# Attention over 32 sequences of different length on one core: hardware loops synchronised by counting registers in place of loop stages with semaphore resets, and one output store per sequence

## The chip, the cores and the metric

The kernel runs on one core of a Trainium2 chip. The metric is the device time of one execution in microseconds (us). Before the change the median of three runs is 631.83 us (626.99 to 632.2 us). One execution was profiled; it took 629.71 us, and the profile's span, from its first to its last instruction, is 627.9 us.

Engines are named as the profile names them: PE is the matrix engine and PEld its weight loads, DVE the vector engine, ACT the scalar engine, POOL the GpSimd engine, SP the engine whose queue here issues all DMA transfers. A name with a q behind it (PEq, SPq) is that engine's sequencer, the part that reads instructions, computes registers and waits on semaphores.

## The reference

```python
batch, max_seq, n_heads, head_dim = (32, 512, 8, 64)
lengths = np.random.randint(64, max_seq, size=batch)
x: [32, 512, 512] float32      w_qkv: [512, 1536] float32

output = np.zeros_like(x)
for b in range(batch):
    seq_len = lengths[b]
    x_b = x[b, :seq_len].copy()
    qkv = np.matmul(x_b, w_qkv)
    q, k, v = np.split(qkv, 3, axis=-1)        # then 8 heads of 64
    ...
    scores = scale * np.matmul(q, k.transpose(0, 2, 1))
    attn = np.exp(scores - scores_max)
    attn = attn / (np.sum(attn, axis=-1, keepdims=True) + 1e-08)
    output[b, :seq_len] = np.matmul(attn, v)   # heads side by side again
```

Every sequence is projected to q, k and v, attended within its own length, and written; rows behind its length are zero in the output.

## The kernel before, in words

**Order of the sequences.** The 32 sequences are ranked on the chip by length, longest first (L59 to L100). A place in that ranking is called a position. A position needs n tiles of 128 rows, n from 4 down to 1. The kernel counts on the chip how many pairs of positions need more than 3, 2 and 1 tiles (`pair_i`, L103 to L112), and it has one hardware loop for each n (L362 and L363), whose first and last pair are read from those counts. With the lengths of this case the loops run 2 iterations at n = 4, 6 at n = 3, 6 at n = 2 and 2 at n = 1, each of them two positions.

**One iteration.** For j = 0 and 1 an iteration merges two lists of steps (L366 to L369): the attention of position 2p+j, and the QKV projection of the position after it, whose x was loaded earlier. The buffers for x, x in 16 bits, its transpose, q, k, v, the output tile and the mask are doubled and alternate with j.

- Projection: POOL casts the n tiles of x to 16 bits (`prep`, L196 to L200), and SP then loads the x of a later position into the freed buffer (L178). PE transposes (L205), ACT copies the transpose out of PSUM (L208), PE multiplies by the weights (L213 for q and k, L230 for v), DVE copies q (L225), k (L221) and v (L237) out of PSUM.
- Attention: DVE copies the position's mask (L262). For each pair of heads and each key tile PE computes scores (L275) and ACT takes their exponentials (L282). For each head PE multiplies by v, which carries a column of ones for the sum (L294), and DVE takes the reciprocal, multiplies it by the row mask and scales the result into the output tile `out_nat` (L302, L303, L306).
- Store (L313 to L317): SP stores the n computed tiles, and for n < 4 stores the remaining 4 - n tiles of the position from a constant tile `zeros`, cleared once by POOL (L155, L156). In the built program the second of these transfers waits until the first has landed. An iteration's last instructions on SP are these two transfers of its position j = 1.

**The loops.** `iteration_sync="staggered"` (L363) cuts a loop body into four stages. Each stage has its own semaphores, which are set back for the next iteration, so that every wait of the body is against a constant. An engine, SP with the transfers of that stage among them, reports that it has left a stage; an engine may enter a stage only when all have left the stage two before it. Between two loops all engines meet at a barrier twice: once when the loop is left, and, after each engine has loaded the next bounds into registers, once before the next is entered.

Of the kernel before, what the change touches and what calls it, by code (L numbers as in the profile page):

```python
# [9 lines left out]
FP32 = mybir.dt.float32  # L10
# [3 lines left out]
ALU = mybir.AluOpType  # L14
AX = mybir.AxisListType

P = 128
# [6 lines left out]
def kernel(  # L24
# [8 lines left out]
    nc = tc.nc  # L33
    B, MAXS, D = x.shape
    NT = MAXS // P
# [5 lines left out]
    const = ctx.enter_context(tc.tile_pool(name="const", bufs=1))  # L41
# [8 lines left out]
    for c in range(NC):  # L50
# [23 lines left out]
        out=cmp,  # L74
        in0=key.unsqueeze(1).broadcast_to([P, B, B]),
        in1=key.unsqueeze(2).broadcast_to([P, B, B]),
        op=ALU.is_gt,
# [5 lines left out]
        out=hit,  # L83
        in0=rank.unsqueeze(1).broadcast_to([P, B, B]),
        in1=idx_f.unsqueeze(2).broadcast_to([P, B, B]),
        op=ALU.is_equal,
    )
    nc.vector.tensor_tensor(
        out=cmp, in0=hit, in1=idx_f.unsqueeze(1).broadcast_to([P, B, B]), op=ALU.mult
# [7 lines left out]
        out=hit, in0=hit, in1=len_f.unsqueeze(1).broadcast_to([P, B, B]), op=ALU.mult  # L97
# [8 lines left out]
    for t in range(1, NT):  # L106
        nc.vector.tensor_scalar(
            out=more[:, t - 1, :], in0=first, scalar1=float(t * P), scalar2=None, op0=ALU.is_gt
# [13 lines left out]
        out=masks[:, 0:B, 1, :],  # L122
        in0=iota_f.unsqueeze(1).broadcast_to([P, B, NT]),
        in1=slen.unsqueeze(2).broadcast_to([P, B, NT]),
        op=ALU.is_lt,
    )
    nc.vector.tensor_scalar(
        out=masks[:, 0:B, 0, :],
        in0=masks[:, 0:B, 1, :],
# [6 lines left out]
    def ring(n, shape, dtype, name, fill=None, pool=const):  # L136
        got = []
        for k in range(n):
            t = pool.tile(shape, dtype, name=f"{name}{k}")
            if fill is not None:  # L140
                nc.gpsimd.memset(t, fill)
            got.append(t)
        return got
# [4 lines left out]
    x_bufs = ring(2, [P, NT, D], FP32, "x_nat")  # L148
    x16_bufs = ring(2, [P, NT, D], F16, "x16")
    xT_bufs = ring(2, [P, NC, MAXS], F16, "xT")  # L150
    o_bufs = ring(2, [P, NT, D], FP32, "out_nat")
    m_bufs = ring(2, [P, 2, NT], FP32, "mask")
    e_bufs = ring(4, [P, 2, NT, MAXS], F16, "et")
    rcp_bufs = ring(4, [P, NT], FP32, "rcp")
    zeros = const.tile([P, NT - 1, D], FP32)  # L155
    nc.gpsimd.memset(zeros, 0.0)  # L156

    g_bufs = ring(2, [P, MAXS], FP32, "g", pool=ps)
    s_bufs = ring(2, [P, 2, MAXS], FP32, "psc", pool=ps)
# [4 lines left out]
    ov = out.rearrange("b (t p) d -> b p t d", p=P)  # L164
# [25 lines left out]
    def qkv_steps(b, n, at):  # L190

        steps = []
        N = n * P
        x16, xT, kT = x16_bufs[b % 2], xT_bufs[b % 2], k_bufs[b % 2]

        def prep():  # L196
            for t in range(n):
                nc.gpsimd.tensor_copy(out=x16[:, t, :], in_=x_bufs[b % 2][:, t, :])  # L198
            if at is not None:
                dma_x(b % 2, at, n)  # L200

        def trans(c):
            pxt = nxt("g", gx_bufs)
            for t in range(n):
                nc.tensor.transpose(  # L205
                    pxt[:, t * P : (t + 1) * P], x16[:, t, c * P : (c + 1) * P], ident_f16
                )
            nc.scalar.copy(out=xT[:, c, 0:N], in_=pxt[:, 0:N])  # L208

        def qk(m):  # L210
            pq = nxt("g", g_bufs)
            for c in range(NC):
                nc.tensor.matmul(  # L213
                    pq[:, 0:N],
                    w_r[:, c, m * P : (m + 1) * P],
                    xT[:, c, 0:N],
                    start=(c == 0),
                    stop=(c == NC - 1),
                )
            if m >= NC:  # L220
                nc.vector.tensor_copy(out=kT[:, m - NC, 0:N], in_=pq[:, 0:N])  # L221
            else:
                for par in range(2):
                    r = slice(HD * par, HD * (par + 1))
                    nc.vector.tensor_copy(out=q_bufs[b % 2][r, m, par, 0:N], in_=pq[r, 0:N])  # L225

        def val(t):
            pv = nxt("g", g_bufs)
            for c in range(NC):
                nc.tensor.matmul(  # L230
                    pv,
                    xT[:, c, t * P : (t + 1) * P],
                    w_r[:, c, 2 * D : 3 * D],
                    start=(c == 0),
                    stop=(c == NC - 1),
                )
            nc.vector.tensor_copy(  # L237
                out=v_bufs[b % 2][:, t, :, 0:HD], in_=pv.rearrange("p (h d) -> p h d", d=HD)
            )

        steps.append(prep)
        for c in range(NC):
            steps.append(lambda c=c: trans(c))
        for m in (0, 4, 1, 5, 2, 6, 3, 7):
            steps.append(lambda m=m: qk(m))
        for t in range(n):
            steps.append(lambda t=t: val(t))
        return steps

    def attn_steps(b, n, at, pos):  # L250

        N = n * P
        kT = k_bufs[b % 2]
        qz = q_bufs[b % 2]
        v_aug = v_bufs[b % 2]
        o_t = o_bufs[b % 2]
        mask = m_bufs[b % 2]
        etp = [None] * (NH // 2)
        steps = []

        def masking():
            nc.vector.tensor_scalar(  # L262
                out=mask,
                in0=masks[:, bass.ds(pos, 1), :, :].rearrange("p o m t -> p (o m) t"),
                scalar1=0.0,
                scalar2=None,
                op0=ALU.add,
            )

        def scores(i, kt):  # L270
            if kt == 0:
                etp[i] = nxt("e", e_bufs)
            psc = nxt("s", s_bufs)
            for par in range(2):
                nc.tensor.matmul(  # L275
                    psc[:, par, 0:N],
                    kT[:, i, kt * P : (kt + 1) * P],
                    qz[:, i, par, 0:N],
                    start=True,
                    stop=True,  # L280
                )
            nc.scalar.activation(  # L282
                out=etp[i][:, :, kt, 0:N],
                in_=psc[:, :, 0:N],
                func=AF.Exp,
                scale=scale,
                bias=mask[:, 0, kt : kt + 1],
            )

        def av(h):  # L290
            pav = nxt("o", pav_bufs)
            for qt in range(n):
                for kt in range(n):
                    nc.tensor.matmul(  # L294
                        pav[:, qt, :],
                        etp[h // 2][:, h % 2, kt, qt * P : (qt + 1) * P],
                        v_aug[:, kt, h, :],
                        start=(kt == 0),
                        stop=(kt == n - 1),
                    )  # L300
            rcp = nxt("r", rcp_bufs)
            nc.vector.reciprocal(out=rcp[:, 0:n], in_=pav[:, 0:n, HD])  # L302
            nc.vector.tensor_tensor(  # L303
                out=rcp[:, 0:n], in0=rcp[:, 0:n], in1=mask[:, 1, 0:n], op=ALU.mult
            )
            nc.vector.tensor_tensor(  # L306
                out=o_t[:, 0:n, h * HD : (h + 1) * HD],
                in0=pav[:, 0:n, 0:HD],
                in1=rcp[:, 0:n].unsqueeze(2).broadcast_to([P, n, HD]),
                op=ALU.mult,  # L310
            )

        def store():  # L313
            to = ov[bass.ds(at, 1), :, :, :].rearrange("o p t d -> (o p) t d")
            nc.sync.dma_start(out=to[:, 0:n, :], in_=o_t[:, 0:n, :])
            if n < NT:
                nc.sync.dma_start(out=to[:, n:NT, :], in_=zeros[:, 0 : NT - n, :])  # L317

        steps.append(masking)
        for i in range(NH // 2):  # L320
            if i > 0:
                got = [lambda kt=kt, i=i: scores(i, kt) for kt in range(n)]
                ave = [lambda h=h: av(h) for h in (2 * i - 2, 2 * i - 1)]
                steps += merge(got, ave)
            else:
                steps += [lambda kt=kt: scores(0, kt) for kt in range(n)]
        steps.append(lambda: av(6))
        steps.append(lambda: av(7))
        steps.append(store)
        return steps  # L330

# [12 lines left out]
    firsts = [0]  # L344
# [15 lines left out]
        step()  # L360

    for k, n in enumerate(range(NT, 0, -1)):  # L362
        with tc.For_i(firsts[k], firsts[k + 1], iteration_sync="staggered") as p:  # L363
            pos = p * 2
            for j in range(2):
                proj = qkv_steps(1 - j, n, batch_at(pos + (3 + j)))  # L366
                att = attn_steps(j, n, batch_at(pos + j), pos + j)
                for step in merge(att, proj):
                    step()  # L369
# [35 lines left out]
```

## Time and profile before

| | |
|---|---|
| median of three runs | 631.83 us (626.99 to 632.2) |
| profiled execution, and its span | 629.71 us, 627.9 us |
| PE busy | 474.2 us, 76% of the span, 4160 matmuls |
| PE weight loads busy | 291.6 us, 46%, 4160 |
| DVE busy | 403.0 us, 64%, 1301 instructions |
| ACT busy | 312.7 us, 50%, 457 |
| POOL busy | 60.9 us, 10%, 99 |
| HBM read and written | 27.30 MB and 33.55 MB, 97 GB/s over the span |
| mean granted PE clock | 0.910 of full speed |

Busy time is an average over a prologue, four loops of different shape and the turns between them. To see what a stage is limited by, the same counts are read for one iteration at a time (a table by stretches of time), and the turns between iterations are read in the timeline, instruction by instruction. The "idle before" of a row is the time in which the engine had nothing to do before it, and the name behind the arrow is what ended it; "issue" means that no wait which the profile shows ended it. The granted clock (PEclk) is the share of full speed at which PE was allowed to run.

### The profile page before, as it was taken

To read this page: it belongs to the slowest core of one execution; us is meant where nothing else is said; L and a number is where in the kernel's file an instruction comes from. 1 tells how busy PE (TensorE), PEld (TensorE's weight loads), DVE (VectorE), ACT (ScalarE), POOL (GpSimd) and SP (SyncE) were. 2 spreads that over 40 slices of the span, in tenths; PEclk is the share of its full clock that TensorE was granted. 3 is DMA by queue.
4 is the path that set the end of the run, shared out by engine and by line. 5 is a ranking of instruction groups with operands and counts; after the bars stand their busy time and mean duration, and the time that the engine had idled before them with its cause. 6 is when DMAs were issued, how large, how long until landed. Compare 5 with 4: busy or idle time off the path is not lost. (4 is left out here: it accounts for less than half of the span.)

```text
span 627.9 us, 12695 instructions
## 1 busy us (share of the span) xinstructions
PE 474.2 (76%) x4160; PEld 291.6 (46%) x4160; DVE 403.0 (64%) x1301; ACT 312.7 (50%) x457; POOL 60.9 (10%) x99
## 2 busy tenths in 40 slices
PE   0187997988796996979969869585968686876675
PEld 0034544544453653545535545363636464554443
DVE  6463764757475773775738837566758595857575
ACT  3107685875573674636636657262725344352321
POOL 8102002000201002002020020011010101010000
PEclk9998998999798897997979979988889798979666
DMA  5313013210411314113121141123232313132243
GB/s 200 140 63 135 20 48 130 71 67 0 170 67 67 100 67 167 55 62 117 67 104 70 60 167 67 67 70 134 100 130 104 134 67 134 67 134 89 96 150 135
DMA packets 30416, 61.06 MB, mean 97 GB/s; under 512 B 1728, under 2 KB 1728, under 8 KB 30400
## 3 DMA queue, kind: packets, MB, share of 16 engines
q1 hardware_dynamic: 30400, 60.86, 26.8%
q8 instruction: 9, 0.15, 0.1%
q14 instruction: 7, 0.06, 0.0%
HBM read 27.30 MB, written 33.55 MB: 97 GB/s over the span
## 5 line engine op out<-in xcount | busy, mean ns | idle before, releaser
L282 ACT ACTIVATE et<-psc,mask 128x768 f16<-128x768 f32 (+3 forms) x320 | 270.8, 870 | 267.7 <-PE psc L275 213.8
L275 PE MATMUL psc<-qz,kT 128*128 128x384 f16 (+3 forms) x640 | 172.1, 351 | 86.9 <-issue 63.0
L213 PE MATMUL g<-xT,w_r 128*128 128x256 f16 (+3 forms) x1056 | 191.2, 312 | 16.0 <-DVE qz L225 12.3
L225 DVE CAST qz<-g 64x384 f16<-64x384 f32 (+3 forms) x264 | 129.9, 492 | 30.7 <-PE g L213 17.6
L213 PEld LDWEIGHTS <-w_r 128*128 128x128 f16 x1056 | 99.9, 102 | 72.2 <-issue 31.8
L294 PE MATMUL pav<-v_aug,et 128*128 128x65 f16 x1792 | 121.3, 199 | 7.1 <-ACT et L282 5.7
L294 PEld LDWEIGHTS <-et 128*128 128x128 f16 x1792 | 99.1, 101 | 47.9 <-ACT et L282 10.0
L275 PEld LDWEIGHTS <-kT 128*128 128x128 f16 x640 | 58.0, 105 | 115.9 <-issue 89.6
L302 DVE RECIPROCAL rcp<-pav 128x3 f32<-128x3 f32 (+3 forms) x256 | 43.0, 171 | 95.7 <-PE pav L294 93.1
L198 POOL CAST x<-x_nat 128x512 f16<-128x512 f32 x84 | 47.9, 612 | 544.1 <-issue 371.1
L230 PE MATMUL g<-w_r,xT 128*128 128x512 f16 x336 | 89.4, 385 | 4.6 <-DVE qz L225 2.5
L306 DVE TENSOR_TENSOR out_nat<-pav,rcp 128x192 f32<-128x192 f32 (+3 forms) x256 | 81.7, 321 | 6.2 <-DVE rcp L302 0.7
L205 PE MATMUL g<-ident_f,x 128*128 128x128 f16 x336 | 53.8, 260 | 33.7 <-POOL x L198 29.6
L208 ACT COPY xT<-g 128x384 f16<-128x384 f16 (+3 forms) x132 | 55.4, 443 | 23.8 <-PE g L205 13.1
L221 DVE CAST kT<-g 128x384 f16<-128x384 f32 (+3 forms) x132 | 64.9, 491 | 3.4 <-PE g L213 0.3
L237 DVE CAST v_aug<-g 128x512 f16<-128x512 f32 x84 | 58.0, 691 | 9.6 <-PE g L230 6.1
L205 PEld LDWEIGHTS <-x 128*128 128x128 f16 x336 | 32.6, 116 | 61.0 <-POOL x L198 42.1
L262 DVE TENSOR_SCALAR mask<-masks 128x8 f32 x32 | 7.3, 269 | 64.1 <-issue 64.0
L230 PEld LDWEIGHTS <-xT 128*128 128x128 f16 x336 | 29.9, 98 | 32.8 <-issue 12.2
L303 DVE TENSOR_TENSOR rcp<-rcp,mask 128x3 f32<-128x3 f32 (+3 forms) x256 | 40.1, 157 | 5.0
L64 DVE CAST len_f<-len 128x32 f32<-128x32 int32 x1 | 8.2, 8248 | 5.3 <-DMA len<-in_lengths_dram 5.3
L53 ACT CAST w_r<-w_f 128x1536 f16<-128x1536 f32 x4 | 5.9, 1472 | 10.4 <-DMA w_f<-in_w_qkv_dram 10.4
(32 smaller groups left out, 25.7 us busy)
## 6 DMA issues: line engine op xcount, KB each, us to landing
x_nat<-in_x_dram SPq DMA_DIRECT2D x12, 768.0 KB, 5.0
out_dram<-out_nat SPq DMA_DIRECT2D x12, 768.0 KB, 3.6
x_nat<-in_x_dram SPq DMA_DIRECT2D x7, 1024.0 KB, 5.4
x_nat<-in_x_dram SPq DMA_DIRECT2D x12, 512.0 KB, 3.8
out_dram<-out_nat SPq DMA_DIRECT2D x12, 512.0 KB, 2.8
out_dram<-zeros SPq DMA_DIRECT2D x12, 512.0 KB, 2.8
out_dram<-out_nat SPq DMA_DIRECT2D x4, 1024.0 KB, 4.4
w_f<-in_w_qkv_dram SPq DMA_DIRECT2D x4, 768.0 KB, 6.1
```

The lines of the kernel that those rows point to most:

```text
L198: nc.gpsimd.tensor_copy(out=x16[:, t, :], in_=x_bufs[b % 2][:, t, :])
L205: nc.tensor.transpose(pxt[:, t * P : (t + 1) * P], x16[:, t, c * P : (c + 1) * P], ident_f16)
L208: nc.scalar.copy(out=xT[:, c, 0:N], in_=pxt[:, 0:N])
L213: nc.tensor.matmul(pq[:, 0:N], w_r[:, c, m * P : (m + 1) * P], xT[:, c, 0:N], start=(c == 0), stop=(c == NC - 1),)
L221: nc.vector.tensor_copy(out=kT[:, m - NC, 0:N], in_=pq[:, 0:N])
L225: nc.vector.tensor_copy(out=q_bufs[b % 2][r, m, par, 0:N], in_=pq[r, 0:N])
L230: nc.tensor.matmul(pv, xT[:, c, t * P : (t + 1) * P], w_r[:, c, 2 * D : 3 * D], start=(c == 0), stop=(c == NC - 1),)
L237: nc.vector.tensor_copy(out=v_bufs[b % 2][:, t, :, 0:HD], in_=pv.rearrange("p (h d) -> p h d", d=HD))
L275: nc.tensor.matmul(psc[:, par, 0:N], kT[:, i, kt * P : (kt + 1) * P], qz[:, i, par, 0:N], start=True, stop=True,)
L282: nc.scalar.activation(out=etp[i][:, :, kt, 0:N], in_=psc[:, :, 0:N], func=AF.Exp, scale=scale, bias=mask[:, 0, kt : kt + 1],)
L294: nc.tensor.matmul(pav[:, qt, :], etp[h // 2][:, h % 2, kt, qt * P : (qt + 1) * P], v_aug[:, kt, h, :], start=(kt == 0), stop=(kt == n - 1),)
L306: nc.vector.tensor_tensor(out=o_t[:, 0:n, h * HD : (h + 1) * HD], in0=pav[:, 0:n, 0:HD], in1=rcp[:, 0:n].unsqueeze(2).broadcast_to([P, n, ...
```

## The change

- All four loops use `iteration_sync="reg_based"`. The semaphores of a loop only count up; nothing is set back within it. What a wait needs is no longer a constant but a number that grows with the iteration, so ahead of a waiting instruction its engine computes that number in a register (a REGISTER_ALU row, or a row of several in one, ISA). At the end of the body each engine raises its base registers. There are no stages, and nothing in the body makes an engine wait for all others.
- In the built program a loop is left through one wait of SP for all transfers under way and one barrier; the second barrier of the turn is gone. The barrier ahead of the first loop is gone too.
- In the body PE's weight loads also count up PE's semaphore, which before only its matmuls did.
- The store is one transfer of all four tiles of `out_nat` for every position. `zeros` and its memset are gone. Ahead of each loop with n < 4 POOL clears tile n of both output buffers (two memsets of 128x512, L367); the tiles above it are clear from the loop before. The bytes stored are the same, 1 MB a position.
- The cast of x on POOL is no longer a copy of one operand but a product of two: x times a column of ones, read again and again along the row (L198 and L199), a tile for which POOL has one small memset (L153).

```diff
+    ones = const.tile([P, 1], FP32)
+    nc.gpsimd.memset(ones, 1.0)
...
-    zeros = const.tile([P, NT - 1, D], FP32)
-    nc.gpsimd.memset(zeros, 0.0)
...
             for t in range(n):
-                nc.gpsimd.tensor_copy(out=x16[:, t, :], in_=x_bufs[b % 2][:, t, :])
+                x32 = x_bufs[b % 2][:, t, :]
+                nc.gpsimd.tensor_tensor(
+                    out=x16[:, t, :], in0=x32, in1=ones.broadcast_to([P, D]), op=ALU.mult
+                )
...
         def store():
-            to = ov[bass.ds(at, 1), :, :, :].rearrange("o p t d -> (o p) t d")
-            nc.sync.dma_start(out=to[:, 0:n, :], in_=o_t[:, 0:n, :])
-            if n < NT:
-                nc.sync.dma_start(out=to[:, n:NT, :], in_=zeros[:, 0 : NT - n, :])
+            nc.sync.dma_start(
+                out=ov[bass.ds(at, 1), :, :, :].rearrange("o p t d -> (o p) t d"), in_=o_t
+            )
...
     for k, n in enumerate(range(NT, 0, -1)):
-        with tc.For_i(firsts[k], firsts[k + 1], iteration_sync="staggered") as p:
+        if n < NT:
+            for o_t in o_bufs:
+                nc.gpsimd.memset(o_t[:, n, :], 0.0)
+        with tc.For_i(firsts[k], firsts[k + 1], iteration_sync="reg_based") as p:
```

Three places of the built program show how the instructions stand. The first is SP at the end of the loop with n = 3: the stores of position j = 0 (`out_nat_143`) and j = 1 (`out_nat_144`). Before:

```order
L315 ISA
L315 DMA out_dram<-out_nat_143 128x3x512
L317 ISA
L317 DMA out_dram<-zeros 128x512
L169 ISA
L169 TENSOR_LOAD order_i
L315 ISA
L315 DMA out_dram<-out_nat_144 128x3x512
L317 ISA
L317 DMA out_dram<-zeros 128x512
L363 REGISTER_ALU
L363 COMPARE_AND_BRANCH
```

and with the change (the lines of the file moved down by up to five):

```order
L317 ISA
L317 DMA out_dram<-out_nat_143 128x4x512
L169 ISA
L169 TENSOR_LOAD order_i
L317 ISA
L317 DMA out_dram<-out_nat_144 128x4x512
L368 ISA
L368 REGISTER_ALU
L368 COMPARE_AND_BRANCH
```

The second transfer of each position, and with it SP's wait for the landing of the first, is gone; two register rows stand ahead of the branch.

The second place is PE at the head of the loop with n = 3: scores (kT weights, `psc`) and the first transposes (x weights, `g`). Before:

```order
L275 MATMUL psc_159<-qz_131,kT_135 128x384
L205 LDWEIGHTS x_140
L205 MATMUL g_157<-ident_f_85,x_140 128x128
L275 LDWEIGHTS kT_135
L275 MATMUL psc_160<-qz_131,kT_135 128x384
```

and with the change:

```order
L278 MATMUL psc_159<-qz_131,kT_135 128x384
L208 REGISTER_ALU
L208 LDWEIGHTS x_140
L208 MATMUL g_157<-ident_f_85,x_140 128x128
L278 REGISTER_ALU
L278 LDWEIGHTS kT_135
L278 MATMUL psc_160<-qz_131,kT_135 128x384
```

The order of the work is the same; a register row stands ahead of the instructions that wait. Of such rows, the one of the loop counter included, a body of PE has 74, 68, 58 and 41 at n = 4, 3, 2 and 1, where it had one.

The third place is DVE in the loop with n = 4: the end of one head's attention (`out_nat`) and the copy of q. Before:

```order
L302 RECIPROCAL rcp_151<-pav_161 128x4
L303 TENSOR_TENSOR rcp_151<-rcp_151,mask_145 128x4
L306 TENSOR_TENSOR out_nat_143<-pav_161,rcp_151 128x4x64
L225 CAST qz_133<-g_157 64x512 x2
L302 RECIPROCAL rcp_152<-pav_162 128x4
```

and with the change:

```order
L305 RECIPROCAL rcp_153<-pav_161 128x4
L306 REGISTER_ALU
L306 TENSOR_TENSOR rcp_153<-rcp_153,mask_147 128x4
L309 REGISTER_ALU
L309 TENSOR_TENSOR out_nat_143<-pav_161,rcp_153 128x4x64
L228 REGISTER_ALU
L228 CAST qz_133<-g_157 64x512 x2
L305 REGISTER_ALU
L305 RECIPROCAL rcp_154<-pav_162 128x4
```

A body of DVE has 70, 68, 63 and 63 such rows, about one ahead of each of its instructions. The order of the work is again the same.

## The prediction

> **What bounds the kernel now.** PE is busy 76% of the span, so I first ask where the other 24% is. The view of waits, grouped by what ended them, names it for the scores' matmul L275, which is the first matmul of every iteration, and for the transfers that SP issues:
>
> ```profile
> PE psc L275 <- issue: 63.0, 13, 5.7
> PE psc L275 <- PEq L363: 17.2, 3, 8.0
> SPq L317 <- DMA out_dram<-out_nat: 57.4, 23, 3.0
> ```
>
> (us in total, times, longest.) There are 16 iterations, and 13 + 3 waits: one at the head of each. PE stands 80.2 us there. The third row is SP between the two transfers of one position. The timeline at one turn of the loop with n = 3 shows what lies in such a wait:
>
> ```profile
> 194.92 1.03 PE L230 MATMUL g<-w_r,xT 128*128 128x512 f16 x4
> 195.98 0.69 DVE L237 CAST v_aug<-g 128x512 f16<-128x512 f32 x1
> 196.59 0.35 DVE L306 TENSOR_TENSOR out_nat<-pav,rcp 128x192 f32<-128x192 f32 x1
> 196.97 0.37 SPq L315 DMA_DIRECT2D out_dram<-out_nat  x1
> 200.53 0.34 SPq L317 DMA_DIRECT2D out_dram<-zeros  x1
> 201.24 2.85 POOL L198 CAST x<-x_nat 128x512 f16<-128x512 f32 x5 [37.86 <-issue]
> 201.51 0.44 DVE L262 TENSOR_SCALAR mask<-masks 128x8 f32 x2 [4.57 <-issue]
> 201.55 0.80 PE L275 MATMUL psc<-qz,kT 128*128 128x384 f16 x2 [5.60 <-issue]
> 202.43 0.90 ACT L282 ACTIVATE et<-psc,mask 128x768 f16<-128x768 f32 x1 [8.92 <-PE psc L275]
> ```
>
> PE ends at 195.95, DVE at 196.94. SP issues the store at 196.97, stands 3.56 us until it has landed, and issues the zeros at 200.53; only then has it left the stage, and POOL, DVE and PE start within 1.1 us of that. Nothing that they then do needs the stored data: the meeting of the stages alone holds them. The chain is DVE's tail (1.0), the store's landing (3.6), SP's report and the restart (1.0).
>
> Within an iteration it is PE, nearly full; the table by stretches (length, then busy PE, PEld, DVE, ACT, POOL, then clock, DMA share, GB/s) shows two bodies, n = 3 and n = 2, the halves of the first, and the last n = 1:
>
> ```profile
> 365.63:401.00 35.37, 33.91 (x304) 20.43 (x304) 25.27 (x78) 23.59 (x32) 3.11 (x6) 0.92 0.22 80
> 365.63:383.80 18.17, 17.96 (x152) 10.71 (x153) 12.29 (x38) 11.90 (x16) 3.11 (x6) 0.85 0.28 98
> 383.80:401.00 17.20, 15.95 (x153) 9.73 (x151) 12.98 (x41) 11.69 (x16) 0.00 (x0) 1.00 0.16 61
> 365.63:372.46 6.83, 6.80 (x48) 3.99 (x49) 1.80 (x8) 5.84 (x10) 3.11 (x6) 0.60 0.59 203
> 553.20:577.73 24.53, 22.20 (x192) 15.37 (x192) 19.20 (x75) 12.49 (x24) 2.04 (x4) 0.88 0.29 106
> 604.53:622.45 17.92, 14.71 (x112) 9.62 (x112) 13.46 (x75) 5.09 (x16) 0.98 (x2) 0.69 0.37 136
> ```
>
> The halves do the same work. The first takes 0.97 us longer; its first 6.83 us run at a granted clock of 0.60, the rest at 1.00. So the gap costs a second time, in the clock behind it.
>
> **The change part by part.**
>
> *The turns lose their meeting (a gain).* At four of the 16 heads a loop is entered; the timeline has these (with SP's last transfers ahead of two):
>
> ```profile
> 27.49 2.28 POOL L198 CAST x<-x_nat 128x512 f16<-128x512 f32 x4 [13.94 <-DMA x_nat<-in_x_dram]
> 49.45 0.59 PE L275 MATMUL psc<-qz,kT 128*128 128x512 f16 x2 [2.22 <-PEq L363]
> 156.45 0.40 SPq L315 DMA_DIRECT2D out_dram<-out_nat  x1
> 160.59 0.80 PE L275 MATMUL psc<-qz,kT 128*128 128x384 f16 x2 [5.57 <-issue]
> 578.99 0.37 SPq L315 DMA_DIRECT2D out_dram<-out_nat  x1
> 584.70 0.60 PE L275 MATMUL psc<-qz,kT 128*128 128x128 f16 x4 [6.97 <-PEq L363]
> ```
>
> Of the 63.0 us, 5.57 is an entry; the 12 turns inside loops hold 57.4. What stays at a turn is a seam. PE's next scores need nothing of DVE's tail, but the first exponential needs the mask, and DVE makes it only behind its tail: 196.94 + 0.2 = 197.1, against the 196.8 at which the first exponential would be due if PE went on at 195.95 (0.88 us later, as 201.55 to 202.43). PE goes on with the next scores and transposes meanwhile. Seam: 0.2 us if all of this is hidden, 1.2 if PE waits for the whole tail and mask; I take 0.7, nearer to what the rows leave. Gain: 57.4 - 12 x 0.7 = **49.0 us** (43.0 to 55.0).
>
> *The slow clock behind each turn goes with the gap (a gain)*, if a seam of under 1 us keeps the clock. Five turns at n = 3, 0.97 each: 4.9. At n = 2 the iterations have no equal halves; their clock of 0.88 over 24.53 us means 24.53 x 0.12 = 2.9 us of clock lost, against 35.37 x 0.08 = 2.8 at n = 3, so I price them the same: 4.9. The single turns at n = 4 and n = 1 hold less, nothing taken. Gain **9.8 us** (4.9 to 9.8).
>
> *The loops' exits now wait for the last store (a loss).* Before, n = 4 was left without it: 156.45 to 160.59 is less than the 4.4 us in which such a store lands. From the landing to PE's first matmul the turn from n = 3 to n = 2 gives 408.99 - 405.59 = 3.40 with two meetings; with one I take 2.6 (3.4 as the bound):
>
> ```profile
> 402.02 0.37 SPq L315 DMA_DIRECT2D out_dram<-out_nat  x1
> 405.59 0.34 SPq L317 DMA_DIRECT2D out_dram<-zeros  x1
> 408.99 0.60 PE L275 MATMUL psc<-qz,kT 128*128 128x256 f16 x2 [7.99 <-PEq L363]
> out_dram<-out_nat SPq DMA_DIRECT2D x4, 1024.0 KB, 4.4
> ```
>
> Every store is 1 MB now. Starts: 156.45 + 4.4 + 2.6 = 163.45 (2.9 later), 402.02 + 7.0 = 409.0 (0), 578.99 + 7.0 = 586.0 (1.3). **+4.2 us** (to +6.6). The second transfer's removal is worth nothing by itself once no turn waits for it; without the loops' change it would be 3.56 us a turn.
>
> *POOL (a loss at entries, hidden elsewhere).* Within a loop POOL idles 37 us between casts, so slower casts hide there; at an entry the first transposes wait.
>
> ```profile
> L198 POOL CAST x<-x_nat 128x512 f16<-128x512 f32 x84 | 47.9, 612 | 544.1 <-issue 371.1
> L156 POOL MEMSET zeros<- 128x1536 f32 x1 | 1.4, 1377 | 0.0
> ```
>
> Two memsets of a third of that one's size are 2 x 0.46 = 0.92 us. No row has a two-input operation on POOL; bounds 0.61 us (as now) and 1.22 (each operand read at the cast's pace); I take 1.1, near the upper, as two operands are read. [...] The last of n casts is then late by 0.92 + n x 0.5: 2.4, 1.9 and 1.4 us for n = 3, 2, 1, 5.7 in all, of which PE's scores ahead of the transposes cover some: **+4** (0.9 to 5.7). In the prologue PE's transposes follow four casts: 4 x 0.5 = +2.0. The barrier ahead of the first loop goes, and of its 2.22 us a seam stays: -1.7. Together **+0.3**. The tail: zeros were issued at 623.38 and land in 3.6, the one store is issued at 621.37 and lands by 625.8: **-1.2**.
>
> ```profile
> 621.37 0.33 SPq L315 DMA_DIRECT2D out_dram<-out_nat  x1
> 623.38 0.38 SPq L317 DMA_DIRECT2D out_dram<-zeros  x1
> out_dram<-zeros SPq DMA_DIRECT2D x4, 768.0 KB, 3.6
> ```
>
> *Register rows (a loss).* Over 16 iterations PE gets 2 x 73 + 6 x 67 + 6 x 57 + 2 x 40 = 970 new rows, DVE about as many. Two places show what one costs and whether it hides: the sequencer rows at the end of the iteration above, and those of DVE at 401:
>
> ```profile
> L363 PEldq EVENT_SEMAPHORE  x1: 51/51/51, 194.5 to 194.5; - x1
> L363 PEldq ALU_OP  x1: 36/36/36, 194.7 to 194.7; - x1
> L363 PEldq COMPARE_BRANCH  x1: 228/228/228, 194.8 to 194.8; - x1
> L363 DVEq ALU_OP  x1: 45/45/45, 401.2 to 401.2; - x1
> 401.04 0.69 DVE L237 CAST v_aug<-g 128x512 f16<-128x512 f32 x1
> L262 DVEq FUSED_REGOPS  x32: 76/78/87, 49.5 to 604.6; - x32
> ```
>
> PE's sequencer takes some 0.1 us a row (194.5, 194.7, 194.8), but it reached the branch 0.9 us before the matmuls ended at 195.95: it runs ahead. DVE's row ran inside a cast. A body of n = 3 has 67 x 0.1 = 6.7 us of new rows on PE's sequencer beside 35.4 us of array work. What is left exposed is a row right behind a wait that has just ended, with no work queued; the cover for all others is the queued matmuls, and without it they cost 97 us. I take 0.4 us an iteration, four such places: **+6** (0 to 15).
>
> *Sum*: -49.0 - 9.8 + 4.2 + 4.0 + 0.3 - 1.2 + 6.0 = -45.5. The profiled execution took 629.7 us, so **584 us**; it lies 2 us under the median, within the spread of the runs. Its own range, with the bounds above added where they can come together, is 570 to 600.
>
> **The rivals.**
>
> *DVE takes over at n = 2 and n = 1.* There DVE is busy 19.20 of 24.53 us and 13.46 of 17.92, with pauses of about 0.03 us between 75 instructions: 21.5 and 15.7. If its 63 new rows did not hide (78 ns each, 4.9 us), 26.4 and 20.6 would be the periods in place of about 23.5 and 18: 6 x 2.9 + 2 x 2.6 = 23 us more. Slower POOL reads beside DVE's would push the same way. Time: 584 - 4 + 23 = 603. For it: full DVE. Against it: the row inside the cast.
>
> *Slower than before: PE's register rows stand in the open.* If a wait on a register keeps the sequencer from running ahead, each of 970 rows costs its 0.1 us: 584 - 6 + 97 = 675. It decides at (584 - 6 to 630) 52 us over 970 rows, 54 ns each. Against it: the branch reached 0.9 us early behind a wait on a constant; no row of before shows a wait on a register.
>
> *Slower than before: the weight loads' count.* 4160 more increments; how many hide?
>
> ```profile
> 399.70 0.44 PE L294 MATMUL pav<-v_aug,et 128*128 128x65 f16 x9
> ```
>
> A load with its matmul takes 49 ns here, one increment included, so another costs between 0 and 49 ns: up to 204 us. It turns the sign at 46 / 4160 = 11 ns. At half the bound, 24 ns, the time is 584 + 100 = 684. Against it: loads overlap matmuls, and over a whole body of n = 3 a pair has 33.91 / 304 = 0.112 us in the mean. [...]
>
> *The engines still meet*, through SP's order or a loop register: gaps of half the size stay, 584 + 25 + 5 = 614.
>
> *All smooth*: seams of 0.2, no exposed row: 584 - 6 - 6 - 2 = 570.
>
> **How the numbers follow.** Forecast (570 to 600) 0.60; all smooth or better 0.08; DVE takes over 0.14; still meeting 0.05; register rows on PE 0.08, of which a quarter lands within 1% of before or under it; weight loads' count 0.05, a fifth likewise. A measurement of this kernel tells about 1% from no change. Faster by over 1%: 0.60 + 0.08 + 0.14 + 0.05 = 0.87, less 0.01 for a worse mix, 0.86; within 1%: 0.03; slower: 0.10 and that 0.01, 0.11. The range: 564 to 614 leaves out the two slower cases and little else.
>
> **What would show it.** Right: L275's wait at a turn at or under 1 us, n = 3 iterations every 35 us (now 201.55 - 160.59 = 41.0), n = 2 every 23.5 (now 553.20 - 408.99 over five, 28.8), a clock near 1.00 inside the loops, entries of 7 to 9 us with casts of about 1.1 us. DVE's case: DVE without idle time at n = 2. PE's cases: bodies of n = 3 longer than 37 us at a clock of 1.00, with idle time ahead of many matmuls (register rows), or L294's nine pairs taking more than 0.44 us (counts). Wrong altogether: gaps of over 2 us at the turns.

## The result, and the profile after

The change makes the kernel faster: 599.6 us (median of four runs, 598.57 to 603.38; two more took 598.51 and 602.07) against 630.2 us, a ratio of 0.953 with a 95% interval of 0.948 to 0.958. The prediction was 584 us with a range of 564 to 614. The direction and the range hold; 15.6 of the 45.5 us that were forecast did not come. The profiled execution is the slowest of the four (603.38 us) and has a span of 600.3 us (before 627.9), so that sums read from its trace come out some microseconds longer than the median.

The waits of PE ahead of the scores, and of the projection's matmul, in the view of waits of the changed kernel (its lines lie up to five further down: L278 was L275, L309 was L306, L216 was L213):

```profile
PE psc L278 <- ACT et L285: 25.6, 38, 1.6
PE psc L278 <- issue: 15.3, 2, 7.8
PE psc L278 <- PEq L368: 8.3, 1, 8.3
PE g L216 <- DVE qz L228: 19.4, 40, 0.9
```

The 13 waits of 63.0 us that ended in "issue" are down to two, which with the third (PEq) are the three entries from loop to loop. The turns within loops no longer show there; what is left of them shows as a wait for ACT's exponentials. The row of L216 is new in size: it was 12.3 us in 36 waits.

The timeline at a turn with n = 3:

```profile
236.33 0.59 PE L233 MATMUL g<-w_r,xT 128*128 128x512 f16 x2
236.76 0.49 PE L278 MATMUL psc<-qz,kT 128*128 128x384 f16 x2
237.65 0.35 DVE L309 TENSOR_TENSOR out_nat<-pav,rcp 128x192 f32<-128x192 f32 x1
237.79 0.34 PE L208 MATMUL g<-ident_f,x 128*128 128x128 f16 x3
237.95 0.48 DVE L265 TENSOR_SCALAR mask<-masks 128x8 f32 x2
238.13 0.40 SPq L317 DMA_DIRECT2D out_dram<-out_nat  x1
238.24 0.90 ACT L285 ACTIVATE et<-psc,mask 128x768 f16<-128x768 f32 x1 [3.57 <-PE g L208]
239.19 0.48 PE L278 MATMUL psc<-qz,kT 128*128 128x384 f16 x2 [1.06 <-ACT et L285]
```

PE goes over the turn without a gap (236.92 is the end of the projection, the next scores began at 236.76), and stands only at 238.13, when both score buffers are full. The chain is DVE's tail (to 238.00), the mask, the exponential. SP's store at 238.13 holds nobody. At n = 2 the same chain is longer:

```profile
471.62 0.29 DVE L309 TENSOR_TENSOR out_nat<-pav,rcp 128x128 f32<-128x128 f32 x1
472.40 0.48 DVE L265 TENSOR_SCALAR mask<-masks 128x8 f32 x2 [0.49 <-DVE out_nat L309]
472.69 0.69 ACT L285 ACTIVATE et<-psc,mask 128x512 f16<-128x512 f32 x1 [8.65 <-DVE mask L265]
473.43 0.38 PE L278 MATMUL psc<-qz,kT 128*128 128x256 f16 x2 [1.56 <-ACT et L285]
```

ACT had been free for 8.65 us and could have started at once; DVE needed 0.49 us of loop registers and branch between its tail and the mask, and PE lost 1.56 us.

How long an iteration takes is read from the table by stretches. The kernel before, four iterations at n = 3 and four at n = 2, each from a loop's second iteration on:

```profile
201.55:365.63 164.08, 135.83 (x1216) 82.04 (x1217) 105.17 (x321) 94.37 (x128) 13.64 (x25) 0.92 0.25 89
437.95:553.20 115.25, 86.00 (x768) 59.74 (x769) 80.61 (x312) 49.91 (x96) 9.23 (x17) 0.91 0.30 109
```

and the changed kernel, with one position j = 1 at n = 3 in the third row:

```profile
198.57:348.80 150.23, 131.40 (x1218) 81.21 (x1217) 110.90 (x321) 94.20 (x128) 24.27 (x24) 0.98 0.29 98
419.37:520.90 101.53, 82.45 (x769) 58.81 (x768) 82.27 (x313) 48.98 (x96) 16.29 (x16) 0.97 0.35 124
255.96:274.12 18.16, 16.08 (x153) 10.01 (x152) 13.84 (x40) 11.73 (x16) 3.03 (x3) 1.00 0.15 58
```

An iteration at n = 3 fell from 41.0 to 37.6 us (forecast: 35), at n = 2 from 28.8 to 25.4 (forecast: 23.5). Two things in these rows were not in the forecast. DVE's busy time in the four iterations at n = 3 grew by 5.7 us, over the same 321 instructions. And position j = 1, in which no turn lies, took 18.16 us at full clock, where before it took 17.20.

The timeline inside that position shows why:

```profile
259.52 3.03 POOL L199 TENSOR_TENSOR x<-x_nat,ones 128x512 f16<-128x512 f32 x3 [10.40 <-PE pav L297]
260.64 0.93 DVE L306 TENSOR_TENSOR rcp<-rcp,mask 128x3 f32<-128x3 f32 x1
262.09 0.48 DVE L306 TENSOR_TENSOR rcp<-rcp,mask 128x3 f32<-128x3 f32 x1
262.88 1.13 DVE L228 CAST qz<-g 64x384 f16<-64x384 f32 x2
264.06 0.81 PE L216 MATMUL g<-xT,w_r 128*128 128x384 f16 x4 [0.72 <-DVE qz L228]
```

DVE's product of reciprocal and row mask, three numbers a row, takes 0.16 us elsewhere. Here, beside POOL's casts (259.52 to 262.55), it took 0.93 and 0.48 us; the second ended with POOL's last cast. DVE is 1.1 us late with its next copies, and PE waits for them.

The turn from the loop n = 4 to n = 3 went as forecast (lines left out):

```profile
152.91 0.40 SPq L317 DMA_DIRECT2D out_dram<-out_nat  x1
159.16 3.04 POOL L199 TENSOR_TENSOR x<-x_nat,ones 128x512 f16<-128x512 f32 x3 [0.21 <-issue]
159.61 0.80 PE L278 MATMUL psc<-qz,kT 128*128 128x384 f16 x2 [8.26 <-PEq L368]
```

From the store to PE's first matmul it is 6.7 us (forecast 4.4 + 2.6 = 7.0).

The last loop, n = 1, did not gain at all. This row reaches from its first matmul to its last store:

```profile
553.72:594.09 40.37, 31.38 (x223) 21.80 (x224) 29.93 (x151) 10.15 (x32) 3.85 (x4) 0.58 0.29 105
```

From the first matmul to PE's last (553.72 to 594.99) the loop takes 41.3 us, where it took 37.7 before (584.70 to 622.41, the turn included), and its clock is 0.58 where an iteration before had 0.69.

### The profile page after: what moved, and what is told of

It reads as the page before. It is cut to its first block, busy times and chain, and to the rows that moved or that the text cites. A ratio compares the mean times of both kernels' runs of the same rounds, so it can differ in the third digit from the quotient of the medians.

```text
span 600.3 us, 14618 instructions
## 1 busy us (share of the span) xinstructions
PE 467.0 (78%) x4160; PEld 292.2 (49%) x4160; DVE 413.9 (69%) x1301; ACT 311.0 (52%) x457; POOL 99.8 (17%) x105
## 5 line engine op out<-in xcount | busy, mean ns | idle before, releaser
L216 PE MATMUL g<-xT,w_r 128*128 128x256 f16 (+3 forms) x1056 | 194.3, 319 | 21.4 <-DVE qz L228 19.4
L278 PE MATMUL psc<-qz,kT 128*128 128x384 f16 (+3 forms) x640 | 158.6, 330 | 50.3 <-ACT et L285 25.6
L216 PEld LDWEIGHTS <-w_r 128*128 128x128 f16 x1056 | 104.2, 104 | 80.4 <-issue 39.2
L199 POOL TENSOR_TENSOR x<-x_nat,ones 128x512 f16<-128x512 f32 x84 | 85.0, 1039 | 300.8 <-PE psc L278 79.2
L278 PEld LDWEIGHTS <-kT 128*128 128x128 f16 x640 | 57.9, 101 | 78.9 <-issue 57.3
L309 DVE TENSOR_TENSOR out_nat<-pav,rcp 128x192 f32<-128x192 f32 (+3 forms) x256 | 81.8, 321 | 4.8
L208 PE MATMUL g<-ident_f,x 128*128 128x128 f16 x336 | 45.4, 232 | 37.7 <-POOL x L199 32.2
L208 PEld LDWEIGHTS <-x 128*128 128x128 f16 x336 | 27.7, 102 | 57.7 <-POOL x L199 36.4
L306 DVE TENSOR_TENSOR rcp<-rcp,mask 128x3 f32<-128x3 f32 (+3 forms) x256 | 52.3, 205 | 4.8
L367 POOL MEMSET out_nat<- 128x512 f32 x6 | 3.0, 524 | 166.9 <-POOLq L405 166.9
```

The lines of the kernel that those rows point to most:

```text
L199: nc.gpsimd.tensor_tensor(out=x16[:, t, :], in0=x32, in1=ones.broadcast_to([P, D]), op=ALU.mult)
L208: nc.tensor.transpose(pxt[:, t * P : (t + 1) * P], x16[:, t, c * P : (c + 1) * P], ident_f16)
L216: nc.tensor.matmul(pq[:, 0:N], w_r[:, c, m * P : (m + 1) * P], xT[:, c, 0:N], start=(c == 0), stop=(c == NC - 1),)
L278: nc.tensor.matmul(psc[:, par, 0:N], kT[:, i, kt * P : (kt + 1) * P], qz[:, i, par, 0:N], start=True, stop=True,)
L309: nc.vector.tensor_tensor(out=o_t[:, 0:n, h * HD : (h + 1) * HD], in0=pav[:, 0:n, 0:HD], in1=rcp[:, 0:n].unsqueeze(2).broadcast_to([P, n, ...
```

## The experiments

Theory A, formed from the rows above: the missing 15 us are POOL's product, which holds up DVE's product of two operands in SBUF, and a seam at the turns that runs through DVE's mask (PE waits 1.06 and 1.56 us in the two shown), with the clock lower behind some of them (0.98 and 0.97 over the four iterations of the rows above). Theory B, the rival: the register rows make bodies and seams longer. Beside these stood the question which part of the change brought the gain.

| run | us | ratio to before (95%) | an iteration, n = 3 | n = 2 |
|---|---|---|---|---|
| before | 630.2 | | 41.0 | 28.8 |
| the change | 599.6 | 0.953 (0.948 to 0.958) | 37.6 | 25.4 |
| e2, mask ahead of the reciprocal | 588.1 | 0.934 (0.931 to 0.937) | 35.2 | 25.2 |
| e3, mask made early | 588.5 | 0.934 (0.930 to 0.937) | 36.1 | 24.4 |
| e4, both | 585.1 | 0.928 (0.925 to 0.932) | 35.5 | 23.6 |
| e5, before with one store | 598.9 | 0.951 (0.948 to 0.954) | 37.2 | 25.9 |
| e6, the change with the old store | 602.7 | 0.959 (0.953 to 0.964) | 36.7 | 25.8 |
| e7, the change in staged loops | 621.5 | 0.988 (0.983 to 0.992) | 39.1 | 27.1 |
| e8, casts on ACT | 592.8 | 0.942 (0.938 to 0.946) | 35.6 | 25.2 |
| e9, casts on ACT, mask early | 595.1 | 0.945 (0.941 to 0.949) | 37.3 | 24.1 |

The iterations are means of four, from a loop's second on, as in the tables by stretches above. Each ratio is to runs of the kernel before that were taken beside it (medians of 629.5 to 630.4 us).

### e2: DVE's product without a second operand in SBUF

```diff
-            nc.vector.reciprocal(out=rcp[:, 0:n], in_=pav[:, 0:n, HD])
-            nc.vector.tensor_tensor(
-                out=rcp[:, 0:n], in0=rcp[:, 0:n], in1=mask[:, 1, 0:n], op=ALU.mult
-            )
+            nc.vector.tensor_tensor(
+                out=rcp[:, 0:n], in0=pav[:, 0:n, HD], in1=mask[:, 0, 0:n], op=ALU.subtract
+            )
+            nc.vector.reciprocal(out=rcp[:, 0:n], in_=rcp[:, 0:n])
```

> The changed kernel, with the row mask applied ahead of the reciprocal: DVE subtracts the mask's -1e30 from the sum in PSUM and then takes the reciprocal, so that no operation of DVE has two operands in SBUF any more (rows behind the length come out as about 1e-30 of their sums in place of 0). Theory A (POOL's product of two operands holds up DVE's product of two SBUF operands, 12 us more busy time there than in the kernel before): the rows that took up to 1.02 us take about 0.16 again wherever POOL is at work, the n = 3 positions j = 1 go from 18.17 back to about 17.2 us, and the time falls by 7 to 10 us to about 591. Theory B (register rows make the bodies longer): nothing changes, 599 to 600.

588.1 us, 11.5 less than the change and somewhat more than A expected. In the table by stretches, the four iterations at n = 3, the four at n = 2, and a position j = 1:

```profile
198.16:339.08 140.92, 127.55 (x1218) 79.27 (x1216) 104.11 (x321) 93.91 (x128) 24.27 (x24) 1.00 0.31 104
407.98:508.82 100.84, 82.89 (x769) 59.78 (x768) 80.38 (x313) 48.60 (x96) 16.30 (x16) 0.95 0.36 125
251.42:268.62 17.20, 15.95 (x153) 9.90 (x152) 12.83 (x40) 11.74 (x16) 3.03 (x3) 1.00 0.16 61
```

and in its timeline the same place as above, in another position:

```profile
254.98 3.03 POOL L199 TENSOR_TENSOR x<-x_nat,ones 128x512 f16<-128x512 f32 x3 [9.17 <-PE pav L297]
255.89 0.16 DVE L305 TENSOR_TENSOR rcp<-pav,mask 128x3 f32<-128x3 f32 x1 [3.32 <-PE psc L278]
256.57 0.15 DVE L305 TENSOR_TENSOR rcp<-pav,mask 128x3 f32<-128x3 f32 x1
```

POOL works as before, DVE's operation takes 0.16 and 0.15 us beside it, and the position takes 17.20 us, to the hundredth what the kernel before took without any of the register rows. That speaks for A and leaves B nothing within a body at n = 3. At n = 2 a position j = 1 takes 11.0 us in e2, and took 16.1 less a turn of 5.0 before, so there is nothing for B there either. Over the whole run this operation's rows are, in the change and in e2:

```profile
L306 DVE TENSOR_TENSOR rcp<-rcp,mask x256: 141/161/1023, 56.7 to 593.5; 128x3 f32<-128x3 f32 x48, 128x2 f32<-128x2 f32 x48, 128x4 f32<-128x4 f32 x16, 128x1 f32<-128x1 f32 x16
```

```profile
L305 DVE TENSOR_TENSOR rcp<-pav,mask x256: 128/151/164, 57.6 to 578.9; 128x3 f32<-128x3 f32 x48, 128x2 f32<-128x2 f32 x48, 128x4 f32<-128x4 f32 x16, 128x1 f32<-128x1 f32 x16
```

(shortest, median, longest in ns.) The longest is 1023 ns in the one and 164 in the other. By the start and end of every row, 37 of the change's 256 products overlap an instruction on POOL, and these take 487 ns in the mean; of the 219 others none takes more than 165. In e2 34 overlap, and take 153 ns in the mean. So beside POOL's product the operation was slow with both operands in SBUF, and not with one of them in PSUM; by what path POOL holds it up no run shows.

### e3: the mask made half an iteration ahead

```diff
-                in0=masks[:, bass.ds(pos, 1), :, :].rearrange("p o m t -> p (o m) t"),
+                in0=masks[:, bass.ds(pos + 2, 1), :, :].rearrange("p o m t -> p (o m) t"),
...
-        steps.append(masking)
...
         steps.append(lambda: av(7))
+        steps.append(masking)
```

and the masks of positions 0 and 1 ahead of the first loop.

> The changed kernel, with each position's mask made by DVE half an iteration ahead (at the end of the position two before it) in place of at the head of the iteration. Theory A (the turn's seam is the chain DVE tail, loop registers of DVE, mask, first exponential): the first exponential of a turn no longer waits for the mask, PE's wait at a turn of 1.2 us at n = 3 and 1.7 us at n = 2 falls to under 0.5, most of the slow-clock windows behind the turns go, and the time falls by 10 to 16 us to about 587. Theory B (register rows set the seam and the bodies): the seam stays over 1 us, and the time falls by under 3 us.

588.5 us, 11.1 less than the change, within what A expected. PE's wait ahead of the scores, 25.6 us in 38 waits with the change (and 24.8 in e2), is now:

```profile
PE psc L278 <- ACT et L285: 6.7, 23, 0.6
```

The table by stretches for the same eight iterations:

```profile
199.77:344.22 144.45, 131.03 (x1218) 79.25 (x1216) 106.13 (x321) 92.47 (x128) 24.28 (x24) 1.00 0.29 102
415.79:513.30 97.51, 83.28 (x770) 57.08 (x769) 81.48 (x313) 48.54 (x96) 16.30 (x16) 1.00 0.36 129
```

The clock is 1.00 in both (0.98 and 0.97 with the change). So PE's wait at the turn ran through the mask, and at n = 2 the slow windows go with it; at n = 3 they are gone in e2 as well, where the wait is still there. What the whole 11.1 us are made of is shown less cleanly. The edit also moves every step of the attention one place ahead in the merged list: at a turn with n = 3 PE now does four matmuls of scores ahead of the first transposes, where it did two. And POOL's casts meet DVE's product in other places, for its 256 rows are busy for 47.3 us in place of 52.3. No run parts the mask from the order.

### e4: both

> Both edits of the two runs before on the changed kernel. Theory A: their gains add up, 17 to 26 us, to about 577. Theory B: within 4 us of the changed kernel, 596 to 600.

585.1 us: 3 less than e2 (the intervals just touch) and 8 short of the sum. Its iterations:

```profile
199.21:341.21 142.00, 132.16 (x1218) 79.17 (x1216) 103.94 (x321) 92.47 (x128) 24.27 (x24) 1.00 0.30 103
412.09:506.49 94.40, 83.01 (x770) 57.74 (x768) 78.47 (x313) 48.54 (x96) 16.30 (x16) 1.00 0.38 133
```

At n = 2 both gains are there: 23.6 us an iteration, against 25.4 with the change and 24.4 in e3. At n = 3 they do not add up: 35.5 us, where e2 alone has 35.2. With the stall gone, the early mask shortens the position with a turn from 18.03 to 17.84 us and lengthens the other from 17.20 to 17.66; the moved steps are one candidate for that, and no run settles it. So at n = 3 most of what e3 gained (37.6 to 36.1) was the stall's, and was counted twice (the product's 256 rows are busy for 52.3 us in the change, 47.3 in e3, and 40.0 in e8 below, where nothing runs on POOL in the loops). Another part was lost in the first passes of the loops, where an engine stands for 2 to 3 us once:

```profile
180.35 0.28 DVE L308 RECIPROCAL rcp<-rcp 128x3 f32<-128x3 f32 x2 [2.40 <-issue]
402.50 0.37 ACT L211 COPY xT<-g 128x256 f16<-128x256 f16 x1 [3.13 <-issue]
```

No wait that the profile shows ended these. e4 is the fastest version that was run; it beats both kernels.

### e5: the kernel before, with the store alone

The staged loops and POOL's copy stay; the two transfers become one, and POOL clears the tails between loops, as in the change.

> The kernel before (staged loops, POOL's cast as a copy), with only the store changed: one transfer of four tiles per position and the tails of the output tiles cleared by POOL between loops. Theory A (the stage is held by SP's standing between its two transfers, not by the landing as such): turns at n = 3 fall from 5.6 to about 2.1 us and at n = 2 from 5.0 to about 2.2, and the time falls by some 30 to 36 us to about 597, as much as the whole change brought. Theory B (the meeting needs the landing in any case, and the gain came from the counting loops): the turns keep 5 us or more, and the time stays within 5 us of 630.

598.9 us: as much as the whole change brought, from its smallest part. A turn with n = 3 in its timeline:

```profile
196.31 0.35 DVE L304 TENSOR_TENSOR out_nat<-pav,rcp 128x192 f32<-128x192 f32 x1
196.78 0.40 SPq L312 DMA_DIRECT2D out_dram<-out_nat  x1
197.75 0.44 DVE L260 TENSOR_SCALAR mask<-masks 128x8 f32 x2 [1.09 <-issue]
197.78 0.48 PE L273 MATMUL psc<-qz,kT 128*128 128x384 f16 x2 [2.12 <-issue]
```

SP leaves the stage once it has issued the store: that was at 196.78, and PE starts at 197.78. PE's gap is 2.12 us in place of 5.60, less by 3.48, which is SP's standing between the two transfers (3.56). The meeting costs the rest: DVE's tail and 1.1 us.

### e6: the change, with the old store

> The changed kernel with only the store undone: counting loops and the product of two operands on POOL, but two transfers per position again, the zeros behind the landing of the computed tiles, and no memsets between loops. Theory A (in counting loops nobody waits for SP at a turn, so that SP may stand between its transfers at no cost): the seams stay 1.2 to 1.7 us; the exits wait for two landings in a row, 3.6 + 2.0 and 2.8 + 2.8 us against 4.4, some 1.2 us more each, and the memsets' 0.9 us each fall away: 598 to 603 us. Theory C (the single store is what makes the time short under either kind of loop): SP's wait shows up in the loads of x and in the turns, 615 us or more.

602.7 us, where A expected it. In counting loops the two transfers cost 3 us, which is not clear of the noise (the intervals overlap), in place of the 31 in staged ones. At a turn SP issues the first transfer and PE goes on, as in the change:

```profile
235.65 0.37 SPq L320 DMA_DIRECT2D out_dram<-out_nat  x1
236.82 0.48 PE L280 MATMUL psc<-qz,kT 128*128 128x384 f16 x2 [1.05 <-ACT et L287]
```

### e7: the change, in staged loops

> The changed kernel with only the kind of loop undone: staged loops, one store, memsets, and the product of two operands on POOL. It stands to the run of the kernel before with the single store (598.9 us) as POOL's product to POOL's copy. Theory A: at every turn all engines start together and PE's first transposes wait for POOL's casts of 1.04 in place of 0.56 us each, up to 1.4 us an iteration at n = 3, 1.0 at n = 2 and 2 us in the prologue, half of it hidden behind scores, and DVE's product is held up where it meets them: 604 to 615 us. If the product costs nothing in staged loops, 597 to 601.

621.5 us, 6 more than the upper end that was expected. Against e5 it differs only in POOL's product, and that costs 22.6 us. The timeline of a turn:

```profile
244.23 4.03 POOL L199 TENSOR_TENSOR x<-x_nat,ones 128x512 f16<-128x512 f32 x4 [32.46 <-issue]
245.32 0.23 PE L208 MATMUL g<-ident_f,x 128*128 128x128 f16 x1 [0.31 <-POOL x L199]
246.32 0.29 PE L208 MATMUL g<-ident_f,x 128*128 128x128 f16 x1 [0.77 <-POOL x L199]
247.32 0.29 PE L208 MATMUL g<-ident_f,x 128*128 128x128 f16 x1 [0.39 <-POOL x L199]
```

In these staged loops POOL has not cast ahead: it starts at 244.23, behind 32.46 us of idle time, and the transposes of one tile after another wait for casts that come a microsecond apart, and the scores that stand behind them in PE's order wait too; little of it was hidden. The stall of DVE's product, which the expectation also reckoned with, has no part in it: the product takes 164 ns at most here, and none of its 256 rows overlaps one of POOL.

### e8 and e9: the casts on ACT

```diff
-                x32 = x_bufs[b % 2][:, t, :]
-                nc.gpsimd.tensor_tensor(
-                    out=x16[:, t, :], in0=x32, in1=ones.broadcast_to([P, D]), op=ALU.mult
-                )
+                nc.scalar.copy(out=x16[:, t, :], in_=x_bufs[b % 2][:, t, :])
```

e9 has e3's edit as well.

> The changed kernel with the casts of x made by ACT, as copies, in place of POOL's product; DVE's product of two SBUF operands is left as it is. Theory A (POOL's product holds up DVE's): with nothing running on POOL in the loops, DVE's product takes 0.16 us everywhere, the n = 3 positions j = 1 go from 18.2 to about 17.2 us, as in the run that took the operand away from DVE's side, and the prologue's casts take about 0.55 us each; ACT idles 2.7 us and more ahead of a position's first exponential, which covers 0.55 x n of casts: 583 to 590 us. If ACT's casts come in the way of the exponentials, positions grow by up to 1.7 us: 595 to 620 us, with DVE's product still at 0.16 us. Theory D (DVE's product is slow for a reason of its own): it keeps its rows of 0.5 to 1.0 us.

> The run with ACT's casts, and each position's mask made half an iteration ahead as well. Theory A: as the run with both edits (585.1 us), less about 1.5 us in the prologue and up to 2 us at the loops' entries, where ACT casts sooner than POOL: 578 to 585 us. With the mask early, ACT's casts no longer lie in a wait at the turn; if they come ahead of the exponentials there, 585 to 600 us.

e8 took 592.8 us. With POOL idle in the loops, the untouched product of DVE is at its short time again:

```profile
L301 DVE TENSOR_TENSOR rcp<-rcp,mask 128x3 f32<-128x3 f32 (+3 forms) x256 | 40.0, 157 | 4.8
```

(205 ns in the change.) So the same stall goes whether DVE's second SBUF operand or POOL's work is taken away. The time is 3 us over the expected range: its iterations are close to those of e2 (35.6 and 25.2 us against 35.2 and 25.2), but the first position at n = 3 took 25.1 us against 20.1 in e2, with one stand of ACT as in e4:

```profile
164.88 1.69 ACT L280 ACTIVATE et<-psc,mask 128x768 f16<-128x768 f32 x2 [3.20 <-issue]
```

e9 took 595.1 us. Its timeline at a turn:

```profile
239.25 0.90 ACT L280 ACTIVATE et<-psc,mask 128x768 f16<-128x768 f32 x1 [2.62 <-PE L203]
240.04 1.12 ACT L196 CAST x<-x_nat 128x512 f16<-128x512 f32 x2
241.07 0.90 ACT L280 ACTIVATE et<-psc,mask 128x768 f16<-128x768 f32 x1
```

With the mask early, ACT's casts lie between its first exponentials, on the chain that PE waits for (n = 3: 37.3 us an iteration). This was the worse of the two cases expected.

One combination was not run: counting loops and one store with POOL's cast left a copy of one operand. In the kernel before, in e5 and in e7 no product of DVE overlaps a row of POOL, so no run here shows whether a copy on POOL would hold it up as the product does, and what the counting loops bring by themselves on top of the single store stays open.

## Why the prediction was right, and where it was wrong

- **What bounds the turn: right.** This is the step on which the forecast of a gain rests. The stage was held by SP's standing between its transfers. e5 takes that away alone and a turn loses 3.48 us of 5.60; e6 shows that counting loops make it harmless just as well. The prediction's sentence that the second transfer's removal would be worth 3.56 us a turn without the loops' change was right, and should have been carried on: two parts of the change remove the same wait, so the smaller of them alone was worth as much as the whole, which had POOL's costs to bear besides.
- **The seam, taken at 0.7 us (0.2 to 1.2): too small at n = 2.** At n = 3 it was right: e2, free of POOL's stall, has 18.03 us for a position with a turn and 17.20 without, 0.83 apart. At n = 2 PE loses 1.56 us, with a stand of DVE of 0.49 us ahead of the mask that the step did not have. The chain itself (tail, mask, exponential) was named rightly: e3 cuts it, and PE's waits there fall from 25.6 to 6.7 us. What cutting it is worth is shown at n = 2 alone; at n = 3 e4 is not shorter than e2.
- **The clock behind a turn: half right.** Of the four middle iterations at n = 3 two ran at a clock of 1.00, and so did two of the four at n = 2; the others ran at 0.93 to 0.96. The condition, a seam of under 1 us, does not decide it: at n = 3 PE waits 1.06 us at a turn of the change and 1.05 at one of e2, whose four iterations are all at 1.00; no run shows a limit. With the mask early it is 1.00 at both.
- **"Within a loop POOL idles 37 us between casts, so slower casts hide there": this step failed.** POOL's own time is hidden, but not what POOL does to DVE meanwhile. In the kernel before, POOL's casts ran only right behind a meeting, and none of DVE's 256 products overlaps one; in counting loops POOL runs ahead, and 37 do. e2 prices it at 11.5 us, from the side of DVE; e8 confirms the place from the side of POOL. It was left in a rival ("slower POOL reads beside DVE's would push the same way") with no price.
- **Register rows, taken at 6 us: nothing that was measured at n = 3 and n = 2.** Position j = 1 at n = 3 takes 17.20 us with and without them. Both slower rivals (rows on PE, the weight loads' count) fall with the same number. A single row (ALU_OP, median in the trace of the change) took 32 ns on PE's weight-load queue and 40 on DVE's, less than the 0.1 us and 78 ns that were reckoned with. DVE's rival fares the same at n = 2, but n = 1 leaves it open: it gave 20.6 us a period, and the two iterations of the change take 41.3. With the same rows single iterations took 18.4 us in e2 and 18.5 in e8 (17.9 before), so the rows alone are not worth 2.7; no run tells how much of the loss at n = 1 is theirs, and how much is the lower clock or POOL.
- **Exits and entries: nearly right, the tail not.** PE's three waits at the entries are 15.3 + 8.3 = 23.6 us (the rows of "issue" and PEq above) against 5.57 + 7.99 + 6.97 = 20.5, so 3.1 more (forecast 4.2). POOL's product takes 1039 ns (forecast 1.1 us). The tail was mis-sized: from PE's last matmul to the end it is 5.3 us against 5.5, where 1.2 us less was forecast, since the last store was issued at 594.05, 0.9 us ahead of PE's end, and no longer two.

The missing 15.6 us, then. At n = 3 an iteration takes 37.6 - 35.1 = 2.5 us more than forecast, 12 in five, which is the stall of DVE (e2: 35.2). At n = 2 it is 25.4 - 23.6 = 1.8, 9 in five, of which the early mask takes 1.0 (e3: 24.4) and the stall the rest (e4: 23.6). At n = 1 the loop is 3.6 longer, where its one turn was to get shorter. Against these stand the 6 that register rows were to cost and did not, a prologue that ends 1.5 us earlier in place of 0.3 later (first matmul at 47.93 in place of 49.45), and the entries. The sum does not close to the microsecond.

That 599.6 us lies at the upper edge of the forecast's own range of 570 to 600 is partly luck: errors of 12, 9 and about 4 us in one direction were met by 6 and some smaller ones in the other. It lies nearer still to the 603 of the rival in which DVE takes over; but DVE was held up by POOL, at n = 3 above all, and not by its register rows at n = 2. e4, which mends the stall and the seam, comes to 585.1 us, where the forecast stood. That too is partly chance, since its first passes lose some microseconds that the forecast did not have.

In sum over the parts, in this order: one store, 630.2 to 598.9; POOL's product on top, to 621.5; counting loops on top, to 599.6. The last step brings 21.9 us, about the 22.6 that POOL's product had cost.

## What to carry to other kernels

When two parts of a change remove the same wait, price each alone: the simpler one may bring it all. When an engine gets the freedom to run ahead, ask not only whether its own time hides but which instructions of others it will now run beside. And put nothing short that the head of an iteration waits for (here a mask of eight numbers) behind the tail of the iteration before.

## What the runs showed of the hardware that was not expected

- DVE's product of reciprocal and row mask, both in SBUF, took up to 1023 ns beside POOL's two-operand product, and 487 in the mean of the 37 that overlap one of POOL's instructions, in place of 157 in the kernel before; with one operand in PSUM DVE's operation took 153 ns in the mean beside the same work of POOL (e2).
- Ahead of DVE's instructions the change has register rows, 40 ns for a single one; in the body at n = 3 one of them ran inside the instruction before it (the row at 260.66 within the product of 260.64, which ended at 261.57). Nothing of them showed in a body at n = 3; at a turn with n = 2 there were 0.49 us between DVE's tail and the mask, with rows of this kind and the branch's.
- In a loop's first pass an engine stood for 2.40 us (e4, DVE) and 3.13 and 3.20 us (ACT in e4 and e8) with no wait shown. In the first of these stretches (e4, 176 to 181) the transfer queues show one packet of 0.01 MB on q14, which the profile calls instruction, and nothing else; whether DVE stood for it no run shows, and why these stands come in e4 and e8 stays open.
